# Two kinds of small product regrouped in a two-layer hybrid attention block: the block compression in four groups of eight, the compressed branch's values in one 128-row product a head

## The chip, the cores and the metric

The kernel runs on one core of a Trainium2 chip. The metric is the device time of one execution in microseconds (us), the median of three runs. The core has five engines with queues of their own: TensorE (PE in the profile, its weight loads shown as PEld), VectorE (DVE), ScalarE (ACT), GpSimd (POOL) and SyncE (SP), which issues nearly all of this kernel's DMAs.

## The reference, cut to what matters

Two layers of width 1024 over 512 tokens, each with two attention mixers, a gated sum of them, and an MLP. The mixer that the change touches is the second one: eight query heads of 64 dimensions in two groups of four, each group with its own keys and values, and three branches whose outputs are added under gates. The first branch attends to compressed keys and values: 31 overlapping blocks of 32 tokens, each put through a two-layer network.

```python
def compress_blocks(t, pos_emb, w1, b1, w2, b2):
    blocks = t[:, :, idx, :] + pos_emb            # 31 blocks of 32 tokens
    flat = blocks.reshape(B, G, nc, CMP_BLOCK * dh)   # 2048 numbers a block
    return jax.nn.gelu(flat @ w1 + b1) @ w2 + b2
...
    s = einsum('bgrqd,bgnd->bgrqn', qi, kc) * scale
    p_c = softmax(where(valid_c, s, NEG_BIG)) * valid_c
    o_c = einsum('bgrqn,bgnd->bgrqd', p_c, vc)
...
    o_n = g[..., 0:1] * o_c + g[..., 1:2] * o_s + g[..., 2:3] * o_w
```

It is done for keys (w1[0]) and for values (w1[1]) of both groups. In the other mixer, the log of the forget gates is summed along the tokens (`cumsum`).

## The kernel before, in words

Activations lie transposed, features on the 128 partitions and the 512 tokens along the free axis. Most products keep float32 accuracy by splitting each operand into a high and a low float32r part and adding three products, high by high, high by low, low by high (`gemm`, L212 to L214). Weights come as 128x1024 float32 chunks by DMA (`fetch`, L170), are split by ScalarE (L186, high) and VectorE (L187, low), and are used in a fixed order, a few chunks ahead.

Attention runs in `attend`: three stages of neighbouring heads are interleaved, scores (L392 and L395, with the softmax's maximum on VectorE, L398, and its exponential on ScalarE, L399), transposes of the probabilities (L421, split by L430 on ScalarE and L431 on VectorE) and products with the values (L447). Between their steps a "fill" generator does other work: in the first mixer, the projections of the next heads and the compression; in the second mixer, the compressed branch's probabilities and the gate projections. So the order in which Python yields decides roughly what lies beside what, and the language's scheduler settles the order on each engine's queue when the program is built. It may also move a DMA issue far ahead, up to the point at which its buffer is free.

Compression (`compress`, L498 to L577). VectorE copies the projected keys and values into tiles `ca` (L506 to L511, L508 writes the position rows). Then 32 products (L525) accumulate in one PSUM bank: for each of 8 steps c, two 256-KB chunks of w1 are loaded (L520, into buffers of the tags `oh` and `ol`, of which there are eight each, shared with the query copies `qx` and with the outputs of finished pairs of heads), and for two values of j and two of i (keys, values) a plain float32 product of 128 rows, 64 columns and 256 moving elements is added: keys to partitions 0 to 63, values to 64 to 127. After each j the generator yields, so that another piece of fill, six products of a projection, comes between. The hidden layer, its GELU and the second layer follow (L532 to L577). The values end as `vc2`, 128 rows (the same 32 blocks four times, one for each head of the group) by 2 groups by 128 columns, high parts in columns 0 to 63 and low parts in 64 to 127 (L576 on ScalarE, L577 on VectorE).

The compressed branch's probabilities (`cmp_probs`) of the four heads of a group come out as one 128x512 tile, row 32r+n for head r and block n: scores L586, transposes L593, the softmax on VectorE and ScalarE (L596 to L608), transposes back L612, and the split into `ch` (L615, ScalarE) and `cl` (L616, VectorE).

Each head of the second mixer ends in `after`: two products (L815) take rows 32r to 32r+31 of `vc2`, against the same rows of `ch` and of `cl`, 32 rows by 128 columns by 512 moving elements each, and add to the head's accumulator, which already holds the other two branches. `out_half` (L458 ScalarE, L459 VectorE) then adds the lower 64 partitions to the upper ones.

Three smaller places. `setup` clears the padded key tile `kcz` on GpSimd (L637). `forget` (L661, L662) sums the gates with float32 products whose moving operand is a 128x128 tile of ones. `go` makes that tile (L1083) and uses it for ten warm-up products as well (L1087).

Of the kernel before, what the change touches and what calls it, by code (L numbers as in the profile page):

```python
# [11 lines left out]
F32 = mybir.dt.float32  # L12
F32R = mybir.dt.float32r
AF = mybir.ActivationFunctionType
# [5 lines left out]
T = 512  # L20
# [123 lines left out]
class Body:  # L144
    def __init__(self, ctx, tc, nc, a):
# [5 lines left out]
        self.dp = P("dp", 1, space=bass.MemoryType.DRAM)  # L151

    BUFS = dict(raw=2, wh=2, wl=2, uh=8, ul=8, oh=8, ol=8, va=4, kd=2, q2=3, vn=1, e=2, t2=12, tmp=3,
                hl=1, r=1, crs=1, small=1, cc=1, s4=6, big=1, kcz=1, vc2=1, g4=2)
# [343 lines left out]
    def compress(self, kc, vc, small, l):  # L498
# [14 lines left out]
            A.append(t)  # L513
            yield
        hp = self.p("O")
        for c in range(8):
            w = []
            for i in range(2):
                raw = self.t(("oh", "ol")[i], [128, T], name="w1")
                nc.sync.dma_start(raw, a["w1"][l, i, c].rearrange("p j m -> p (j m)"))  # L520
                w.append(raw)
            for j in range(2):
                jj = 2 * c + j
                for i in range(2):
                    nc.tensor.matmul(hp[64 * i:64 * i + 64, :256], A[i][jj // 8][:, jj % 8],  # L525
                                     w[i][:, j * 256:(j + 1) * 256], start=jj == 0, stop=jj == 15)
                yield
        h = self.t("tmp", [128, 256])
        nc.scalar.copy(h, hp[:, :256])
        pt = self.p("S")  # L530
# [41 lines left out]
        b2v = small[:, OFF["b2v"]:OFF["b2v"] + 64]  # L572
        for hk in range(2):
            nc.vector.scalar_tensor_tensor(v[:, hk], pv[:, hk * 64:hk * 64 + 64], 0.5, b2v, op0=OP.mult, op1=OP.add)
        self.vc2 = self.t("vc2", [128, 2, 128], F32R)
        nc.scalar.copy(self.vc2[:, :, :64], v)  # L576
        nc.vector.tensor_sub(self.vc2[:, :, 64:], v, self.vc2[:, :, :64].bitcast(F32))  # L577

    def cmp_probs(self, hk, q2):

        nc = self.nc
        sc = self.p("S")
        for r in range(4):
            q = q2[2 * hk + r // 2][:, r % 2]
            for f in range(2):
                nc.tensor.matmul(sc, self.kcz[:, hk, f, 96 - 32 * r:224 - 32 * r], q,  # L586
                                 start=r == 0 and f == 0, stop=r == 3 and f == 1)
        s = self.t("tmp", [128, T])
        nc.scalar.copy(s, sc)
        pt = self.p("PT")  # L590
        for b in range(NB):
            sl = slice(b * 128, (b + 1) * 128)
            nc.tensor.transpose(pt[:, sl], s[:, sl], self.ident)  # L593
# [12 lines left out]
        gt = self.gates[:, :, 0, 4 * hk:4 * hk + 4]  # L606
        nc.vector.tensor_mul(z.rearrange("p (b r) -> p b r", b=NB), z.rearrange("p (b r) -> p b r", b=NB), gt)
        nc.vector.tensor_mul(x3, x3, z[:, :, None].to_broadcast([128, 16, 32]))  # L608
        pt = self.p("PT")
        for b in range(NB):  # L610
            sl = slice(b * 128, (b + 1) * 128)
            nc.tensor.transpose(pt[:, sl], x[:, sl], self.ident)  # L612
        h = self.t("t2", [128, T], F32R, name="ch")
        lo = self.t("t2", [128, T], F32R, name="cl")
        nc.scalar.copy(h, pt)  # L615
        nc.vector.tensor_sub(lo, pt, h.bitcast(F32))  # L616
        self.pc[hk] = (h, lo)
        yield

    BUFS.update(s16=2)  # L620
# [18 lines left out]
    def forget(self, z):  # L639

# [65 lines left out]
    def layer(self, l, u):  # L706
# [99 lines left out]
        def nsa_units(h):  # L806
# [2 lines left out]
            O = [None]  # L809

            def after():
                ph, pl = self.pc[hk]
                s = slice(32 * r, 32 * r + 32)
                for f, t in enumerate((ph, pl)):
                    nc.tensor.matmul(O[0], self.vc2[s, hk], t[s], start=False, stop=f == 1)  # L815
# [262 lines left out]
    def go(self):  # L1078
        nc, a = self.nc, self.a
        self.gain = self.cp.tile([128, 40], F32, name="gain")  # L1080
        nc.sync.dma_start(self.gain, a["gain"])
        self.ones = self.cp.tile([128, 128], F32, name="ones")
        nc.vector.memset(self.ones, 1.0)  # L1083
        self.ones2 = self.ones[:, :2]
        ps = self.p("PT")
        for _ in range(self.WARM):
            nc.tensor.matmul(ps[:, :128], self.ones, self.ones, start=True, stop=True)  # L1087
        warm = self.t("s4", [128, 1], name="warm")
        nc.scalar.activation(warm, self.ones[:, :1], AF.Exp)
# [211 lines left out]
```

## Time and profile before

| | us |
|---|---|
| median of three runs | 1553.21 (1552.73 to 1553.71) |
| the profiled execution | 1552.95 |
| span of the program in it | 1551.2 |
| outside the span | 1.75 |

The profile is of one execution. Its first part gives each engine's busy time. The other views used below are the chain of work that ended last, the table of who waited for whom, the timeline of single engines (start, length, engine, line, output and inputs, shape, how many merged), the instructions of one line (shortest, median and longest duration in ns), and busy times by stage. A matrix product's length in the timeline reaches over the start of the next one, since products are pipelined, so its cost on TensorE is read from one start to the next. A plain float32 product appears as two records, a float32r product as one.

### The profile page before, as it was taken

Reading aid. Unit: us, or ns where it says so; the run is one execution under the profiler, and the core shown is the slowest. Engines: PE = TensorE matmul, PEld = TensorE weight load, DVE = VectorE, ACT = ScalarE, POOL = GpSimd, SP = SyncE. Lnnn points to the kernel's source line nnn. Section 1 sums busy time; section 2 is a strip of 40 time slices with the busy share of each in tenths; the row PEclk is TensorE's granted clock in tenths of the full one; section 3 lists DMA queues with packets and bytes.
Section 4 is the critical chain, followed back from the end, with each engine's and each line's share of the span. In section 5 each row is a group of like instructions: output and inputs, shape, how many; then the busy total and the mean of one; then the engine's idle time right before and its main releaser. Section 6 shows DMA issues by size and latency. Waiting matters only on the chain.

```text
span 1551.2 us, 22739 instructions
## 1 busy us (share of the span) xinstructions
PE 1536.4 (99%) x8460; PEld 1306.6 (84%) x8460; DVE 1075.2 (69%) x2204; ACT 776.0 (50%) x1455; POOL 205.2 (13%) x177
## 2 busy tenths in 40 slices
PE   9999999999999999999999999999999999999997
PEld 8877888888888999999887688888888889999997
DVE  5687988766569776664646789887664887766643
ACT  6444655553454555444433456555434635545553
POOL 4000000000201232221400000000002013222222
PEclk9999999999999999999999999999999999999999
DMA  7545422133333322321535543221433333323131
GB/s 240 172 128 154 127 82 82 55 114 117 96 95 123 109 96 95 109 82 64 176 117 165 157 140 100 68 82 55 150 95 95 95 120 99 113 91 99 65 96 55
DMA packets 56638, 169.57 MB, mean 109 GB/s; under 512 B 7344, under 2 KB 8112, under 8 KB 56528
## 3 DMA queue, kind: packets, MB, share of 16 engines
q1 hardware_dynamic: 53072, 161.84, 33.5%
q10 hardware_dynamic: 3456, 6.29, 1.2%
q8 instruction: 66, 1.08, 0.3%
q14 instruction: 44, 0.36, 0.1%
HBM read 140.77 MB, written 4.19 MB: 93 GB/s over the span
## 4 chain that ended last, share of the span: by engine, by line
PE 95%; DVE 3%; ACT 1%; issue 1%; POOL 0%; DMA 0%; DVEq 0%; SPq 0%; POOLq 0%; ACTq 0%
PE ps_mm L212 12%; PE ps_mm L213 12%; PE ps_mm L214 12%; PE ps_S L1196 4%; PE ps_O L1196 4%; PE ps_O L447 4%; PE ps_mm L1196 3%; PE ps_PT L421 3%; PE ps_PT L1196 3%; PE ps_S L212 3%; PE ps_S L213 3%; PE ps_S L214 3%; PE ps_PT L212 3%; PE ps_PT L213 3%; PE ps_PT L214 3%; PE ps_O L212 3%
## 5 line engine op out<-in xcount | busy, mean ns | idle before, releaser
L186 ACT CAST wh<-raw 128x1024 fp32r<-128x1024 f32 (+2 forms) x187 | 192.6, 1030 | 263.7 <-issue 58.5
L187 DVE TENSOR_TENSOR wl<-raw,wh 128x1024 fp32r<-128x1024 f32 (+2 forms) x187 | 226.6, 1212 | 49.8 <-ACT wh L186 48.9
L212 PE MATMUL ps_mm<-uh,wh 128*128 128x512 f32 x512 | 205.1, 401 | 0.0
L214 PE MATMUL ps_mm<-uh,wl 128*128 128x512 f32 x512 | 202.3, 395 | 0.0
L213 PE MATMUL ps_mm<-ul,wh 128*128 128x512 f32 x512 | 202.1, 395 | 0.0
L399 ACT ACTIVATE E<-E,mx 128x128 f32<-128x128 f32 x192 | 108.0, 563 | 82.7 <-DVE mx L398 75.6
L430 ACT CAST pth<-ps_PT 128x512 fp32r<-128x512 f32 x144 | 73.0, 512 | 94.7 <-PE ps_PT L421 94.4
L212 PEld LDWEIGHTS ps_mm<-uh,wh 128*128 128x128 f32 x512 | 96.2, 188 | 26.5 <-issue 10.6
L214 PEld LDWEIGHTS ps_mm<-uh,wl 128*128 128x128 f32 x512 | 96.2, 188 | 20.4 <-issue 0.8
L213 PE MATMUL ps_mm<-ol,wh 128*128 128x512 f32 (+1 forms) x288 | 111.5, 387 | 1.5 <-POOL ol L1263 1.5
L212 PE MATMUL ps_mm<-oh,wh 128*128 128x512 f32 (+1 forms) x288 | 111.8, 388 | 0.0
L214 PE MATMUL ps_mm<-oh,wl 128*128 128x512 f32 (+1 forms) x288 | 111.2, 386 | 0.0
L398 DVE CUSTOM_DVE_ANT_0 E<-ps_S,ct 128x128 f32<-128x128 f32 x192 | 92.2, 483 | 26.5 <-PE ps_S L395 25.0
L213 PEld LDWEIGHTS ps_mm<-ul,wh 128*128 128x128 f32 x512 | 96.4, 188 | 15.1
L431 DVE TENSOR_TENSOR ptl<-ps_PT,pth 128x512 fp32r<-128x512 f32 x144 | 85.0, 595 | 27.6 <-ACT pth L430 27.2
L1187 DVE TENSOR_TENSOR sl<-s,sh 128x512 fp32r<-128x512 f32 x96 | 76.6, 801 | 36.6 <-ACT sh L1186 36.3
L1263 POOL TENSOR_TENSOR ol<-c,oh 128x512 fp32r<-128x512 f32 x48 | 62.7, 1306 | 295.9 <-ACT oh L1262 268.3
L1186 ACT CAST sh<-raw 128x512 fp32r<-128x512 f32 x72 | 44.7, 620 | 106.3 <-PE ps_S L1196 48.1
L1186 ACT CAST sh<-s 128x512 fp32r<-128x512 f32 x96 | 59.3, 620 | 56.4 <-PE ps_PT L1196 19.3
L253 POOL TENSOR_TENSOR acc<-sq 128x512 f32<-128x512 f32 (+1 forms) x6 | 8.4, 1394 | 595.0 <-DVE wl L187 580.1
L421 PE MATMUL ps_PT<-ct,E 128*128 128x128 f32 x480 | 82.9, 273 | 1.4 <-DVE ptl L431 1.4
L421 PEld LDWEIGHTS ps_PT<-ct,E 128*128 128x128 f32 x480 | 60.1, 140 | 14.8 <-DVE ptl L431 4.2
(441 smaller groups left out, 4068.0 us busy)
## 6 DMA issues: line engine op xcount, KB each, us to landing
raw<-wb SPq DMA_DIRECT2D x64, 512.0 KB, 3.2
raw<-wup SPq DMA_DIRECT2D x64, 512.0 KB, 3.7
raw<-wd SPq DMA_DIRECT2D x48, 512.0 KB, 3.5
kd<-hl SPq DMA_DIRECT2D x48, 256.0 KB, 4.6
w<-w SPq DMA_DIRECT2D x32, 256.0 KB, 5.8
q<-hl SPq DMA_DIRECT2D x64, 128.0 KB, 3.2
raw<-wo SPq DMA_DIRECT2D x16, 512.0 KB
raw<-wout SPq DMA_DIRECT2D x16, 512.0 KB, 3.6
```

The costliest lines, as they stand in the source:

```text
L186: nc.scalar.copy(h[:, :n], raw[:, :n])
L187: nc.vector.tensor_tensor(lo[:, :n], raw[:, :n], h[:, :n].bitcast(F32), op=OP.subtract)
L212: mm(ps, h[:, c], xh, start=start and i == 0, stop=False)
L213: mm(ps, h[:, c], xl, start=False, stop=False)
L214: mm(ps, lo[:, c], xh, start=False, stop=stop and i == ks - 1)
L398: nc.vector.tensor_tensor_reduce(e, ps[:, :n], self.mask[:, T - n:], -1.0, BIG, OP.add, OP.min, mx)
L399: nc.scalar.activation(e, e, AF.Exp, bias=mx, scale=-1.0, accum_out=sm[:, i:i + 1])
L421: nc.tensor.transpose(ps[:, j * 128:(j + 1) * 128], E[i][:, b * 128:(b + 1) * 128], self.ident)
L431: nc.vector.tensor_sub(lo[:, o:o + n], ps[:, :n], h[:, o:o + n].bitcast(F32))
L1186: nc.scalar.copy(h, src)
L1187: nc.vector.tensor_tensor(lo, src, h.bitcast(F32), op=OP.subtract)
L1196: self.nc.tensor.matmul(ps, w, x, skip_group_check=True, **kw)
```

## The change

It does four things.

1. In `compress`, the chunks of w1 are loaded two steps ahead, and the products come in four groups of eight (two steps c at a time: four j, two i each) without a yield inside a group. The number of yields is the same as before, 16.
2. The compressed values go into a tile `vz` of 128 rows by 2 groups by 2 by 128 columns that is cleared once on GpSimd. Of its two versions, one holds the value rows of heads 0 and 2 of a group and zeros between, the other those of heads 1 and 3. Four copies on ScalarE and four subtractions on VectorE of 32 partitions each write it, in place of one and one of 128 partitions.
3. The probabilities are split into two tiles of 128 rows in place of `ch` and `cl`: in the first, rows 0 to 63 are the high parts of heads 0 and 1 and rows 64 to 127 their low parts; in the second it is heads 2 and 3, with the halves the other way round. Two copies and two subtractions of 64 partitions write them, in place of one and one of 128. So each head needs one product of 128 rows, where it had two of 32 rows.
4. The 128x128 tile of ones is no longer kept. The warm-up uses a passing one, and `forget` reads one column of ones, repeated 128 times by a zero stride.

```diff
+        loaded = deque()
+
+        def load(c):
+            for i in range(2 if c < 8 else 0):
                 raw = self.t(("oh", "ol")[i], [128, T], name="w1")
                 nc.sync.dma_start(raw, a["w1"][l, i, c].rearrange("p j m -> p (j m)"))
-                w.append(raw)
-            for j in range(2):
+                loaded.append(raw)
+
+        load(0)
+        load(1)
+        for c in range(0, 8, 2):
+            load(c + 2)
+            yield
+            load(c + 3)
+            yield
+            w = [loaded.popleft() for _ in range(4)]
+            for j in range(4):
                 jj = 2 * c + j
                 for i in range(2):
                     nc.tensor.matmul(hp[64 * i:64 * i + 64, :256], A[i][jj // 8][:, jj % 8],
-                                     w[i][:, j * 256:(j + 1) * 256], start=jj == 0, stop=jj == 15)
-                yield
+                                     w[j // 2 * 2 + i][:, j % 2 * 256:(j % 2 + 1) * 256],
+                                     start=jj == 0, stop=jj == 15)
+            yield
+            yield
...
-        self.vc2 = self.t("vc2", [128, 2, 128], F32R)
-        nc.scalar.copy(self.vc2[:, :, :64], v)
-        nc.vector.tensor_sub(self.vc2[:, :, 64:], v, self.vc2[:, :, :64].bitcast(F32))
+        for k in range(4):
+            s = slice(32 * k, 32 * k + 32)
+            z = self.vz[s, :, k % 2]
+            nc.scalar.copy(z[:, :, :64], v[s])
+            nc.vector.tensor_sub(z[:, :, 64:], v[s], z[:, :, :64].bitcast(F32))
...
-        h = self.t("t2", [128, T], F32R, name="ch")
-        lo = self.t("t2", [128, T], F32R, name="cl")
-        nc.scalar.copy(h, pt)
-        nc.vector.tensor_sub(lo, pt, h.bitcast(F32))
-        self.pc[hk] = (h, lo)
+        self.pc[hk] = []
+        for f in range(2):
+            c = self.t("t2", [128, T], F32R, name="cp")
+            s, o = (slice(64 * e, 64 * e + 64) for e in (f, 1 - f))
+            nc.scalar.copy(c[s], pt[s])
+            nc.vector.tensor_sub(c[o], pt[s], c[s].bitcast(F32))
+            self.pc[hk].append(c)
...
+        self.vz = self.cp.tile([128, 2, 2, 128], F32R, name="vz")
+        nc.gpsimd.memset(self.vz.bitcast(F32), 0.0)
...
-                nc.tensor.matmul(ps[:8, s], p[:, k * 8:(k + 1) * 8], self.ones, start=k == 0, stop=False)
+                nc.tensor.matmul(ps[:8, s], p[:, k * 8:(k + 1) * 8], self.ones2[:, :1].to_broadcast([128, 128]), start=k == 0, stop=False)
...
-                ph, pl = self.pc[hk]
-                s = slice(32 * r, 32 * r + 32)
-                for f, t in enumerate((ph, pl)):
-                    nc.tensor.matmul(O[0], self.vc2[s, hk], t[s], start=False, stop=f == 1)
+                nc.tensor.matmul(O[0], self.vz[:, hk, r % 2], self.pc[hk][r // 2], start=False, stop=True)
...
-        self.ones = self.cp.tile([128, 128], F32, name="ones")
-        nc.vector.memset(self.ones, 1.0)
-        self.ones2 = self.ones[:, :2]
+        self.ones2 = self.cp.tile([128, 2], F32, name="ones")
+        nc.vector.memset(self.ones2, 1.0)
+        ones = self.t("tmp", [128, 128], name="ones")
+        nc.vector.memset(ones, 1.0)
...
-            nc.tensor.matmul(ps[:, :128], self.ones, self.ones, start=True, stop=True)
+            nc.tensor.matmul(ps[:, :128], ones, ones, start=True, stop=True)
```

More of the change, by code (lines that the diff above doesn't have):

```diff
@@ L153 @@
     BUFS = dict(raw=2, wh=2, wl=2, uh=8, ul=8, oh=8, ol=8, va=4, kd=2, q2=3, vn=1, e=2, t2=12, tmp=3,
-                hl=1, r=1, crs=1, small=1, cc=1, s4=6, big=1, kcz=1, vc2=1, g4=2)
+                hl=1, r=1, crs=1, small=1, cc=1, s4=6, big=1, kcz=1, g4=2)
     def t(self, tag, shape, dt=F32, name=None):
@@ L515, in compress @@
         hp = self.p("O")
-        for c in range(8):
-            w = []
-            for i in range(2):
+        loaded = deque()
+        def load(c):
+            for i in range(2 if c < 8 else 0):
                 raw = self.t(("oh", "ol")[i], [128, T], name="w1")
                 nc.sync.dma_start(raw, a["w1"][l, i, c].rearrange("p j m -> p (j m)"))
-                w.append(raw)
-            for j in range(2):
+                loaded.append(raw)
[8 more added lines that the diff above has]
+            for j in range(4):
                 jj = 2 * c + j
@@ L1081, in go @@
         nc.sync.dma_start(self.gain, a["gain"])
-        self.ones = self.cp.tile([128, 128], F32, name="ones")
-        nc.vector.memset(self.ones, 1.0)
-        self.ones2 = self.ones[:, :2]
+        self.ones2 = self.cp.tile([128, 2], F32, name="ones")
+        nc.vector.memset(self.ones2, 1.0)
+        ones = self.t("tmp", [128, 128], name="ones")
+        nc.vector.memset(ones, 1.0)
         ps = self.p("PT")
         for _ in range(self.WARM):
-            nc.tensor.matmul(ps[:, :128], self.ones, self.ones, start=True, stop=True)
+            nc.tensor.matmul(ps[:, :128], ones, ones, start=True, stop=True)
         warm = self.t("s4", [128, 1], name="warm")
-        nc.scalar.activation(warm, self.ones[:, :1], AF.Exp)
+        nc.scalar.activation(warm, ones[:, :1], AF.Exp)
         self.xs = [self.dp.tile([128, T], F32, name=f"xs{k}") for k in range(KT)]
```

## The prediction

> **What bounds the kernel now.** I read the page first (busy times, then the chain that ended last), and after it the table of what TensorE waited for.
>
> ```profile
> PE 1536.4 (99%) x8460; PEld 1306.6 (84%) x8460; DVE 1075.2 (69%) x2204; ACT 776.0 (50%) x1455; POOL 205.2 (13%) x177
> ...
> PE 95%; DVE 3%; ACT 1%; issue 1%; POOL 0%; DMA 0%; DVEq 0%; SPq 0%; POOLq 0%; ACTq 0%
> ```
>
> ```profile
> PE ps_mm L213 <- POOL ol L1263: 1.5, 2, 1.1
> PE ps_O L525 <- DVE ca L511: 1.4, 2, 0.7
> PE ps_PT L421 <- DVE ptl L431: 1.4, 2, 0.7
> ```
>
> TensorE makes up 95% of the chain, and the longest waits that end its idle time add up to a few microseconds in the whole span; the rows left out are shorter. So the kernel is a queue of products, and time on TensorE that goes away, goes from the end, as long as nobody else becomes late. The two last rows lie in the compression, once a layer, and come back below. A busy share of 99% hides something, though: what a product costs is the distance from its start to the next start, and around the changed products that distance is longer than elsewhere.
>
> **The values of the compressed branch (L815).** The timeline of TensorE around one head:
>
> ```profile
> 216.38 0.39 PE L213 MATMUL ps_mm<-ul,wh 128*128 128x512 f32 x1
> 216.61 0.39 PE L214 MATMUL ps_mm<-uh,wl 128*128 128x512 f32 x1
> 216.93 0.49 PE L815 MATMUL ps_O<-ch,vc 32*128 32x512 f32 x1
> 217.26 0.39 PE L815 MATMUL ps_O<-cl,vc 32*128 32x512 f32 x1
> 217.58 0.50 PE L212 MATMUL ps_mm<-uh,wh 128*128 128x512 f32 x1
> 217.92 0.40 PE L213 MATMUL ps_mm<-ul,wh 128*128 128x512 f32 x1
> ```
>
> Two 128-row products of 512 columns are 0.23 us apart (216.38 to 216.61). The product ahead of the 32-row pair takes 0.32 to the next start, the pair 0.33 and 0.32, and the product behind it 0.34 (217.58 to 217.92). A head therefore costs 0.09 + 0.65 + 0.11 = 0.85 us. The changed kernel has one 128-row product of the same 512 columns with no change of shape around it: 0.23. It saves 0.62 a head, and with 16 heads in two layers **9.9 us**. As the weights are zero in 64 of the rows, the sum is the same; that zeros cost nothing extra follows from the shape, which is that of the rows beside it.
>
> The Trainium skill speaks against this edit ("TensorEngine Tiling (Array Packing)", Theoretical Speedup): with 32 rows the array splits in four, for a speedup of up to 4. If the two 32-row products ran beside each other they would cost about the 0.23 of one, and the edit would save only the 0.20 around them, 3.2 us. The trace decides otherwise here: both use the same 32 rows, and they start 0.33 us apart.
>
> **The compression products (L525).** One unit of today, both i of one j, in its place:
>
> ```profile
> 94.82 0.39 PE L214 MATMUL ps_mm<-uh,wl 128*128 128x512 f32 x1
> 95.14 0.65 PE L525 MATMUL ps_O<-w,ca 128*64 128x256 f32 x4
> 95.72 0.50 PE L212 MATMUL ps_mm<-uh,wh 128*128 128x512 f32 x1
> 96.05 0.39 PE L213 MATMUL ps_mm<-ul,wh 128*128 128x512 f32 x1
> ...
> 118.00 0.39 PE L213 MATMUL ps_mm<-ul,wh 128*128 128x512 f32 x1
> 118.32 1.08 PE L525 MATMUL ps_O<-w,ca 128*64 128x256 f32 x6
> 119.33 0.50 PE L214 MATMUL ps_mm<-uh,wl 128*128 128x512 f32 x1
> ...
> 120.77 0.65 PE L525 MATMUL ps_O<-w,ca 128*64 128x256 f32 x2
> 121.34 0.50 PE L395 MATMUL ps_S<-kd,qx 128*128 128x512 f32 x1
> 121.68 0.28 PE L447 MATMUL ps_O<-pth,vf 128*128 128x256 f32 x1
> ```
>
> Entry +0.09 (0.32 in place of 0.23), the unit 0.58 (95.14 to 95.72), exit +0.10 (0.33 in place of 0.23): 0.77. What the group looks like is read from two rows. A unit of four records (both i) and one of two records (one i alone, 120.77) take 0.57 to 0.58 alike, so the two i, which write different halves of the columns, run side by side. The row of six records is one unit and one more product: 1.01 to the next start, so one more product behind the first costs 0.43, with entry and exit paid once. If the two i also run side by side further in, a group of four j costs 0.58 + 3 x 0.43 + 0.19 = 2.06, and four groups **8.2 us** a layer.
>
> Today's cost of a layer: 12 undisturbed units at 0.78 (9.4) and one half unit at 117.08 like them (0.8); the stretch 118.00 to 121.68, 3.68 less four 512-column products at 0.23, is 2.8 (one such product and a half unit stand in the rows left out); and the first unit, which stands in a stall:
>
> ```profile
> 86.38 0.40 PE L214 MATMUL ps_mm<-uh,wl 128*128 128x512 f32 x1
> 86.70 0.65 PE L525 MATMUL ps_O<-w,ca 128*64 128x256 f32 x2
> 88.03 0.55 PE L421 MATMUL ps_PT<-ct,E 128*128 128x128 f32 x3 [0.68 <-DVE ptl L431]
> 88.33 0.48 PE L395 MATMUL ps_S<-kd,qx 128*128 128x256 f32 x2
> 89.53 0.65 PE L525 MATMUL ps_O<-w,ca 128*64 128x256 f32 x2 [0.71 <-DVE ca L511]
> 90.11 0.39 PE L447 MATMUL ps_O<-pth,vf 128*128 128x256 f32 x1
> ```
>
> 86.38 to 90.11 is 3.73, of which the other products need 0.8 and L447 behind pays 0.1: 3.0. Together 9.4 + 0.8 + 2.8 + 3.0 = 16.0. In the order of the changed program (read from the built program, no time is in it) all four groups stand unbroken, and the first comes two dozen projection products later, so the wait for `ca` goes. The wait for `ptl` stays and grows: L421 still cannot start before 88.03, and TensorE now arrives at 86.61, so 1.4 us of idle time stand where 0.6 of product stood. Saved: 16.0 - 8.2 - 1.4 = 6.4 a layer, **12.8 us** in two.
>
> **What is added beside it.** The smaller pieces, by form, from the instructions of single lines:
>
> ```profile
> L577 DVE TENSOR_TENSOR vc<-tmp,vc x2: 278/278/278, 148.1 to 913.0; 128x128 fp32r<-128x128 f32 x2
> L616 DVE TENSOR_TENSOR cl<-ps_PT,ch x4: 692/694/694, 187.9 to 1025.7; 128x512 fp32r<-128x512 f32 x4
> L459 DVE TENSOR_TENSOR o<-ps_O,tmp x32: 673/689/695, 94.5 to 1120.9; 64x512 f32<-64x512 f32 x32
> ```
>
> L459 does 64 partitions in the 0.69 us in which L616 does 128, so halving or quartering the partitions shortens nothing. VectorE gets 3 x 0.28 + 2 x 0.69 = 2.2 us a layer more. ScalarE gets as many instructions more, and is busy half the time. All of it is hidden if VectorE has room. By stage:
>
> ```profile
> 138.00:160.00 22.00, 22.00 (x117) 18.41 (x115) 20.26 (x58) 9.26 (x21) 0.00 (x0) 1.00 0.53 149
> 160.00:200.00 40.00, 40.00 (x219) 33.81 (x218) 38.17 (x101) 26.83 (x61) 0.00 (x0) 1.00 0.38 106
> ```
>
> The columns are length, then busy time of PE, PEld, DVE, ACT and POOL. Between 138 and 200 VectorE is busy 58.4 of 62 us, and 0.8 (`vz`) plus 0.7 (the first group of heads) fall just there: 59.9 of 62. That still fits, barely. The built order makes one thing late there: between the transposes L593 and L612, the program now puts 16 projection products where there are 25.
>
> ```profile
> 179.13 0.66 PE L593 MATMUL ps_PT<-ct,tmp 128*128 128x128 f32 x4
> ...
> 186.65 0.60 PE L612 MATMUL ps_PT<-ct,tmp 128*128 128x128 f32 x4
> ```
>
> ```profile
> 185.47 0.68 DVE L608 TENSOR_TENSOR tmp<-tmp,s 128x512 f32<-128x512 f32 x1
> ```
>
> TensorE reaches L612 7.5 us after L593 today; nine products at 0.23 less make that 5.5, while the softmax on VectorE ends at 186.15, 7.0 after L593, and its order there is unchanged. So TensorE waits 1.5 us, in both layers: **+3.0 us**. The bounds are 0 (if L593 itself comes later against VectorE's work) and 6 (if the whole of VectorE's added 1.5 also shows).
>
> The rest at nothing, with bounds. The w1 loads are as many as before:
>
> ```profile
> w<-w SPq DMA_DIRECT2D x32, 256.0 KB, 5.8
> ```
>
> Twelve instead of eight are issued before the projections' weights in each layer, 1 MB more, in a place where SyncE waits for free buffers anyway; a late chunk would show as a wait of TensorE, and I allow 1 us a layer. Clearing `vz` is one more instruction among the clears at the start, on an engine that is busy 13%. The products in `forget` read a repeated column; there are six a layer, of two records each. No row shows a repeated moving operand. I take no change, since the shape is the same. At worst twice as slow, it would be 24 x 0.11 = 2.6 us, with the step of the L421 records above, which also have 128 columns (three take 0.30, 88.03 to 88.33).
>
> **The sum.** -9.9 - 12.8 + 3.0 = -19.7. The profiled execution took 1552.95, 0.26 less than the median of the runs, so I forecast 1552.95 - 19.7 + 0.26, that is **1533.5**.
>
> **The rivals.**
> 1. VectorE becomes the bound of the stretch 138 to 200 in each layer. For it: 59.9 of 62. Against: TensorE waits for nobody there now. If the added 2.2 us a layer show in full on top of the wait at L612, it costs 4.4, and with 1 us a layer for products that meet a busy VectorE after the compression has shrunk, 6.4: 1538 to 1540. Chance 0.25.
> 2. The wait at L612 does not come, since the scheduler's shift of those nine products only moves them ahead of L593: 1530.5, and with the whole `ptl` wait of 2 x 1.4 hidden as well, 1528. Chance 0.18.
> 3. The change doesn't do what it says: inside a group the two i stop running side by side, since nothing in the trace shows a second pair directly behind a first. Each group is then 0.58 + 7 x 0.43 + 0.19 = 3.8, four of them 15.1, and the compression saves -0.5 a layer instead of 6.4: 1547. Against it: in the row of six, the third product starts while the order alternates i. Chance 0.05.
> 4. Slower than before: TensorE, which takes its queue in order, stands at the fourth group for the last four chunks of w1, since SyncE issues these behind the query copies of the third pair of heads. They are first issued about 6 us after that projection ends and land about 6 later, and the group stands some 25 us behind the projection, by the order and 0.23 a product. Each microsecond beyond the 13 of slack costs 2 in all; it outweighs the saving from 10 us beyond it. The chunks would have to take four times today's 5.8. Chance 0.02.
>
> **How the numbers follow.** The forecast (1531 to 1537) has 0.47, rival 1 has 0.25, rival 2 0.18, rival 3 0.05, rival 4 0.02, and 0.03 is left for an order whose stalls eat the gain. The range from 1528 to 1541 takes in the forecast, rivals 1 and 2, and the bounds of the repeated column; what it leaves out is under 0.2. A change of 0.2%, 3.1 us, is about what a measurement of this kernel can tell from none. Faster by more than that: the first four, 0.95. Same 0.02, slower 0.03.
>
> **What would show it.** The value products: 16 of 128 rows, each 0.23 from start to start, no 0.32 ahead. The compression: four rows of 16 records a layer, about 1.87 to the next start; 3.6 would be rival 3. A wait of TensorE (or its weight loads) at L612 of about 1.5, twice; at L421 of 1.4, twice; none for `ca`. VectorE at 96% or more between 138 and 200 with waits of TensorE on L398 or L431 is rival 1. The forecast is wrong if the stretch from 86 to 138 shrinks by less than 5 us.

## The result and the profile after

| | before | after |
|---|---|---|
| median, us | 1553.46 (4 runs, 1552.73 to 1553.89) | 1544.12 (4 runs, 1543.45 to 1546.21) |
| the profiled execution, us | 1552.95 | 1544.18 |
| its span, us | 1551.2 | 1542.1 |

The ratio is 0.9943, with a 95% interval of 0.9925 to 0.996. The kernel is 9.3 us faster. The forecast was 1533.5, within 1528 to 1541: the sign was right, but of the 19.7 us that it expected less than half came, and the time lies outside the range.

The page of the changed kernel has the same two lines as that of before, busy times and chain:

```profile
PE 1520.6 (99%) x8444; PEld 1307.0 (85%) x8444; DVE 1078.6 (70%) x2215; ACT 779.9 (51%) x1465; POOL 207.8 (13%) x178
...
PE 91%; DVE 6%; ACT 2%; issue 1%; DMA 1%; POOL 0%; DVEq 0%; SPq 0%; POOLq 0%; ACTq 0%
```

TensorE's busy time fell by 15.8 us, the span by 9.1. The difference went to waits: TensorE's part of the chain fell from 95% to 91%, and VectorE's rose from 3% to 6%. The table of TensorE's waits in the changed kernel (total, times, longest) says at which lines:

```profile
PE ps_mm L212 <- DVE gate L854: 3.1, 2, 1.5
PE ps_PT L421 <- DVE ptl L431: 2.5, 2, 1.2
PE ps_S L392 <- DVE mx L398: 1.8, 4, 0.6
...
PE ps_S L601 <- DMA q<-hl: 0.4, 1, 0.4
```

The wait for `ca` is gone. The waits for `ptl` grew from 1.4 to 2.5. New are the waits for the gate (3.1), for the maxima L398 (1.8), and some shorter ones, of which the one for a DMA is shown.

The products themselves are what the forecast said. TensorE's timeline of the changed kernel, around the first group of the compression (L535, formerly L525), around one head's value product (L831, formerly L815), at L566, behind the compression's hidden layer (L554 before), and at the transposes L627 (L612 before):

```profile
94.00 0.39 PE L214 MATMUL ps_mm<-uh,wl 128*128 128x512 f32 x1
94.32 1.95 PE L535 MATMUL ps_O<-w,ca 128*64 128x256 f32 x16
96.20 0.50 PE L212 MATMUL ps_mm<-uh,wh 128*128 128x512 f32 x1
96.53 0.40 PE L213 MATMUL ps_mm<-ul,wh 128*128 128x512 f32 x1
...
138.71 0.55 PE L566 MATMUL ps_S<-G,small 128*128 128x64 f32 x3 [0.15 <-DVE G L556]
...
184.17 0.60 PE L627 MATMUL ps_PT<-ct,tmp 128*128 128x128 f32 x4
...
214.32 0.39 PE L214 MATMUL ps_mm<-uh,wl 128*128 128x512 f32 x1
214.55 0.40 PE L831 MATMUL ps_O<-cp,vz 128*128 128x512 f32 x1
214.78 0.39 PE L212 MATMUL ps_mm<-uh,wh 128*128 128x512 f32 x1
```

A group is one row of 16 records and 1.88 to the next start (94.32 to 96.20), with 0.09 ahead and 0.10 behind: 2.07 where 2.06 was forecast. The value product costs 0.23 (214.55 to 214.78). So neither product is the reason.

Where the time comes and goes is read by comparing the starts of the same product in both kernels. In the kernel before, L554 is here:

```profile
143.44 0.66 PE L554 MATMUL ps_S<-G,small 128*128 128x64 f32 x4
```

The compression stage of the first layer has therefore gained 143.44 - 138.71 = 4.7 us, where 6.4 were forecast. At the transposes L612 (186.65 before, 184.17 now) the lead is down to 2.5, at the end of the layer's attention it is 4.4, and in the second layer the same happens once more, to 9.1 at the end of the span. The second mixer, which was to bring 4.95 - 1.5 a layer, brings about nothing.

### The profile page after: what moved, and what is told of

It reads as the page before. It is cut to its first block, busy times and chain, and to the rows that moved or that the text cites. A ratio compares the mean times of both kernels' runs of the same rounds, so it can differ in the third digit from the quotient of the medians.

```text
span 1542.1 us, 22729 instructions
## 1 busy us (share of the span) xinstructions
PE 1520.6 (99%) x8444; PEld 1307.0 (85%) x8444; DVE 1078.6 (70%) x2215; ACT 779.9 (51%) x1465; POOL 207.8 (13%) x178
## 4 chain that ended last, share of the span: by engine, by line
PE 91%; DVE 6%; ACT 2%; issue 1%; DMA 1%; POOL 0%; DVEq 0%; SPq 0%; POOLq 0%; ACTq 0%
PE ps_mm L212 11%; PE ps_mm L213 11%; PE ps_mm L214 11%; PE ps_S L1213 4%; PE ps_O L1213 4%; PE ps_O L447 4%; PE ps_mm L1213 3%; PE ps_PT L1213 3%; PE ps_PT L421 3%; PE ps_S L212 3%; PE ps_S L213 3%; PE ps_S L214 3%; PE ps_PT L212 3%; PE ps_PT L213 3%; PE ps_PT L214 3%; PE ps_O L213 3%
## 5 line engine op out<-in xcount | busy, mean ns | idle before, releaser
L212 PE MATMUL ps_mm<-uh,wh 128*128 128x512 f32 x512 | 203.1, 397 | 0.0
L430 ACT CAST pth<-ps_PT 128x512 fp32r<-128x512 f32 x144 | 73.0, 511 | 91.8 <-PE ps_PT L421 91.4
L212 PE MATMUL ps_mm<-oh,wh 128*128 128x512 f32 (+1 forms) x288 | 111.9, 389 | 3.2 <-DVE gate L854 3.1
L212 PEld LDWEIGHTS ps_mm<-uh,wh 128*128 128x128 f32 x512 | 96.3, 188 | 18.0 <-ACT E L399 1.5
L398 DVE CUSTOM_DVE_ANT_0 E<-ps_S,ct 128x128 f32<-128x128 f32 x192 | 91.4, 481 | 22.5 <-PE ps_S L395 21.6
L431 DVE TENSOR_TENSOR ptl<-ps_PT,pth 128x512 fp32r<-128x512 f32 x144 | 85.0, 593 | 26.4 <-ACT pth L430 25.8
L421 PE MATMUL ps_PT<-ct,E 128*128 128x128 f32 x480 | 85.2, 275 | 2.9 <-DVE ptl L431 2.5
L421 PEld LDWEIGHTS ps_PT<-ct,E 128*128 128x128 f32 x480 | 60.3, 141 | 17.9 <-DVE ptl L431 5.5
```

The costliest lines, as they stand in the source:

```text
L212: mm(ps, h[:, c], xh, start=start and i == 0, stop=False)
L398: nc.vector.tensor_tensor_reduce(e, ps[:, :n], self.mask[:, T - n:], -1.0, BIG, OP.add, OP.min, mx)
L421: nc.tensor.transpose(ps[:, j * 128:(j + 1) * 128], E[i][:, b * 128:(b + 1) * 128], self.ident)
L431: nc.vector.tensor_sub(lo[:, o:o + n], ps[:, :n], h[:, o:o + n].bitcast(F32))
```

## The experiments

**The theories.** A: the loss comes from the pieces that the two splits add (eight instructions of 32 partitions for the values, two and two of 64 for each group's probabilities), although VectorE had room for their time. Its rival B puts the loss elsewhere: into what the regrouped compression brings on behind it, or into the value products themselves. The first three kernels take the change apart. All medians below stand beside runs of the kernel before on the same chip, whose medians were 1553.28 to 1553.66.

### Each part alone

The first kernel is before with the new loop of `compress` only (the diff of that function, nothing else).

> Only the four groups of eight, with the values as in the kernel before. The trace of the changed kernel shows the compression stage 5.0 us a layer shorter, and 5.4 us a layer lost again in the second mixer. Theory A (the added instructions of the split, on VectorE and ScalarE, delay what TensorE waits for): without them the loss in the second mixer is at most the 1.7 us wait behind the compressed softmax, so 10.0 - 3.4 = 6.6 to 10 us faster than before. Theory B (the loss comes with the products' new places: TensorE is early and meets VectorE's chain, and the order of the second mixer is settled anew): the loss is here too, 4 to 5 us a layer, so 0 to 2 us faster.

Measured: 1543.73 (1543.55 to 1545.18), ratio 0.9941 [0.9928, 0.9953], 9.6 faster: as fast as the whole change. In it the lead of 4.7 us at the end of the compression stands unchanged through the second mixer. So the loss behind the compression isn't the compression's doing. Its table of waits already holds two of the three new rows, with the same numbers: 2.5 for `ptl` and 1.8 for the maxima.

The second is the changed kernel with the loop of before in `compress`.

> Only the 128-row value product, its split and the ones; the compression as before. Products save 0.59 us x 16 = 9.4 us. Theory A: the split's instructions cost about 3.7 us a layer, so 2 us faster than before. Theory B: the order of the second mixer stays nearly that of before, so 8 to 9 us faster.

Measured: 1553.26 (1552.76 to 1554.36), ratio 1.0 [0.9991, 1.0009]. The value part, forecast at 9.9 less 3.0, gains nothing at all, less even than the 2 us that theory A left it. It has the third new row:

```profile
PE ps_mm L212 <- DVE gate L842: 3.1, 2, 1.5
```

The third is before, with the splits cut and the products unchanged:

```diff
-        nc.scalar.copy(self.vc2[:, :, :64], v)
-        nc.vector.tensor_sub(self.vc2[:, :, 64:], v, self.vc2[:, :, :64].bitcast(F32))
+        for k in range(4):
+            s = slice(32 * k, 32 * k + 32)
+            nc.scalar.copy(self.vc2[s, :, :64], v[s])
+            nc.vector.tensor_sub(self.vc2[s, :, 64:], v[s], self.vc2[s, :, :64].bitcast(F32))
...
-        nc.scalar.copy(h, pt)
-        nc.vector.tensor_sub(lo, pt, h.bitcast(F32))
+        for f in range(2):
+            s = slice(64 * f, 64 * f + 64)
+            nc.scalar.copy(h[s], pt[s])
+            nc.vector.tensor_sub(lo[s], pt[s], h[s].bitcast(F32))
```

> The kernel before with all its products, but the split of the compressed values written by four plus four instructions of 32 partitions, and that of the probabilities by two plus two of 64, as in the changed kernel: the added instructions alone. Theory A: 4 to 7 us slower than before. Theory B: within 1 us of before.

Measured: 1559.28 (1558.9 to 1559.92), ratio 1.0039 [1.0026, 1.0051], 6.0 slower, with the gate's wait:

```profile
PE ps_mm L212 <- DVE gate L842: 3.1, 2, 1.6
```

The cut alone costs 6.0 us without any of the new products: A stands, and B falls for the regrouping. VectorE got 4.4 us of instructions more; the cut costs more than its own time. ScalarE got as many pieces more, and no kernel here tells its pieces from VectorE's by moving them.

### Which of the two splits, and by what

In the built program the order of TensorE's queue differs between these kernels. Between the transposes L593 and L612 of the first group of heads stand 33 products in the kernel before, and 24 in the changed kernel and in both kernels above that have the gate's wait. So A has two forms. A1: the pieces matter by the order that they lead to. A2: by their time on VectorE. Four kernels: before with only the values' split cut (first half of the diff above), before with only the probabilities' split cut (second half), the changed kernel with whole instructions for `vz`, and the changed kernel with VectorE's four pieces moved to GpSimd (`nc.gpsimd.tensor_sub`).

> The kernel before, with only the split of the compressed values cut in four pieces of 32 partitions (four copies on ScalarE and four subtractions on VectorE in place of one of each); the result and all products are the same. It adds 3 x 0.28 = 0.84 us a layer on VectorE, and in the built order 24 products instead of 33 stand between the transposes of the scores (L593) and those of the probabilities (L612) of the first group of heads, as in the changed kernel; behind the other group it is 29 in both. Theory A1 (the loss hangs on the order that these pieces lead to: TensorE arrives early at L612 and waits there for the gates' row, 1.5 us a layer, and arrives early behind it): 3.5 to 5 us more than before, 1557 to 1558.5, with a wait of TensorE for the gate of 3 us in all. Theory A2 (each added instruction costs its own time on a full VectorE, whatever the order): 1.7 more, 1555. Theory B (the split is not the cause): 1553.

Measured: 1557.27 (1556.74 to 1557.97), ratio 1.0026 [1.0016, 1.0036]: 3.8 slower, as A1 has it and more than twice the 1.7 of VectorE's time. Its table has `PE ps_mm L212 <- DVE gate L840` with 3.1, twice.

> The kernel before, with only the split of the probabilities cut in two halves of 64 partitions (two copies and two subtractions a group in place of one of each); the result and all products are the same. It adds 2 x 0.69 = 1.4 us a layer on VectorE; between L593 and L612 of the first group stand 33 products in the built order, as before. Theory A1 (the order decides): 0 to 2 us more than before, 1553.3 to 1555.5, without a wait for the gate. Theory A2 (each added instruction costs its own time): 2.8 more, 1556. Theory B: 1553.

Measured: 1556.84 (1556.09 to 1557.33), ratio 1.002 [1.0011, 1.0029]: 3.4 slower, which is A2's 2.8 and a little, and A1's forecast missed. The gate's wait is not there. The one row of its table that belongs to the second mixer's new work:

```profile
PE ps_PT L593 <- ACT tmp L589: 0.2, 1, 0.2
```

The waits are too short for the table, but the starts of the same products in both kernels show where the time goes. L612 starts at 186.65 before and at 187.04 here, a transpose L421 behind it at 193.85 before and at 195.03 here: 0.8 us are lost in these 7 us. Behind the second group of heads it is 0.5, and the second layer loses the same again at the same places. That is right behind the pieces, and about as much as one piece of 0.69 on VectorE for each group, as A2 has it. But TensorE's order changes there too (from 188.9 on), and ScalarE has a piece more as well, so which of the three makes the loss is open.

The masked version, with `zm` a 128x2 tile that holds a one where the version has its rows and a zero elsewhere, set once on GpSimd:

```diff
-        for k in range(4):
-            s = slice(32 * k, 32 * k + 32)
-            z = self.vz[s, :, k % 2]
-            nc.scalar.copy(z[:, :, :64], v[s])
-            nc.vector.tensor_sub(z[:, :, 64:], v[s], z[:, :, :64].bitcast(F32))
+        for e in range(2):
+            z, m = self.vz[:, :, e], self.zm[:, e:e + 1]
+            nc.scalar.activation(z[:, :, :64], v, AF.Copy, scale=m)
+            nc.vector.scalar_tensor_tensor(z[:, :, 64:], v, m, z[:, :, :64].bitcast(F32), op0=OP.mult, op1=OP.subtract)
```

> The changed kernel, but the two versions of the compressed values are written whole: each by one copy on ScalarE with a column of ones and zeros as its scale and one scalar-tensor-tensor on VectorE (value times the column, less the high part) over 128 partitions, two and two instructions in place of four and four, and no clearing of the tile. The same products as the changed kernel; 32 of them stand between L593 and L612 of the first group in place of 24. Theory A1: the gate's wait goes and with it about 2.5 us a layer; 1538 to 1541. Theory A2: half of the added pieces goes, 2 x 2 x 0.28 = 1.1 less, 1543. Theory B (the 128-row value products lose their gain themselves, or give it back at the end of each head): 1544, with the gate's wait gone and others in its place.

Measured: 1539.7 (1539.4 to 1540.06), ratio 0.9913 [0.99, 0.9927]: 4.4 less than the changed kernel, as A1 has it; A2's 1.1 alone is out. Its table has no row for the gate and begins with the 2.5 for `ptl` and the 1.8 for the maxima. So 3.1 of the 4.4 us are the gate's wait.

> The changed kernel, with the four subtractions that write the low parts of the compressed values on GpSimd in place of VectorE (all operands lie in SBUF). VectorE loses 4 x 0.28 = 1.1 us a layer; 26 products in place of 24 stand between L593 and L612 of the first group in the built order, so the order stays nearly that of the changed kernel. Theory A1 (order): the gate's wait stays for the most part, 1.0 to 1.5 a layer; 1542 to 1544. Theory A2 (VectorE's time): 2.2 less, 1542, and with VectorE freed of more than the cut added 1541. Theory B: 1544.

Measured: 1545.24 (1543.98 to 1545.52), ratio 0.9946 [0.9933, 0.9958]. VectorE is freed of all four pieces, more than the values' cut added there, and nothing is gained; the median is 1.1 us above the changed kernel's, above all three forecasts. (That it is slower isn't shown: the profiled run has a single wait of 1.5 us of TensorE, at 873 us, for which the profile shows no releaser, and two of the five runs took 1543.98.) 26 products stand between the transposes, and the wait stays, shorter by the two products that came back (2 x 0.23 in each layer):

```profile
PE ps_mm L212 <- DVE gate L854: 2.2, 2, 1.1
```

So for the values' split A1 holds: with 24 or 26 products between the transposes TensorE arrives before the gate, and with 32 or 33 it does not. The pieces' time on VectorE has no part in this wait, since VectorE ends the gate equally late behind the transposes in every kernel. The first transposes, the gate on VectorE, and the product L212 that waits for it or not, in the kernel before (its transposes start at 179.13), in the changed kernel (transposes alone) and in the masked version:

```profile
184.87 0.68 DVE L838 TENSOR_TENSOR gate<-ps_mm,R 128x512 f32<-128x512 f32 x1
```

```profile
176.91 0.64 PE L608 MATMUL ps_PT<-ct,tmp 128*128 128x128 f32 x4
```

```profile
174.82 0.66 PE L607 MATMUL ps_PT<-ct,tmp 128*128 128x128 f32 x4
...
180.56 0.68 DVE L857 TENSOR_TENSOR gate<-ps_mm,R 128x512 f32<-128x512 f32 x1
...
181.62 0.39 PE L212 MATMUL ps_mm<-oh,wh 128*128 128x512 f32 x1
```

VectorE ends the gate 6.42 us behind the start of the first transposes before, 6.42 in the masked version, and 6.40 in the changed kernel (182.63 + 0.68 - 176.91, from the rows further down); in all the other kernels it is 6.4 as well. TensorE's products up to L212 fill 7.06 us before and 6.80 in the masked version, but only 4.76 in the changed kernel (181.44 + 0.23 - 176.91), where it stands until the gate is done.

### The value products without the cut

The changed kernel with whole instructions for both splits, to see what the products alone are worth. It leaves out the second version of `vz` and the pairing of high with low parts, so its products multiply the wrong rows; their number, shape and place are those of the changed kernel:

```diff
-        for k in range(4):
...
+        z = self.vz[:, :, 0]
+        nc.scalar.copy(z[:, :, :64], v)
+        nc.vector.tensor_sub(z[:, :, 64:], v, z[:, :, :64].bitcast(F32))
...
+        nc.scalar.copy(h, pt)
+        nc.vector.tensor_sub(lo, pt, h.bitcast(F32))
+        self.pc[hk] = (h, lo)
```

> The changed kernel with the splits as they were before: one copy and one subtraction of 128 partitions each for the compressed values (into the first version of the cleared tile; the second stays zero) and for the probabilities. The products are the same in number, shape and place, one of 128 rows a head; what they multiply is not the right pair of parts, so the compressed branch's output is left wrong in this kernel and only its time is read. 33 products stand between L593 and L612, as before. Theory A1 (the value products gain their 0.6 a head, and the pieces of the two splits and the order they lead to take it back): grouped compression and values in full, 1543.7 - 9.4 = 1534.3; 1533 to 1536. Theory B (the products lose the gain at the end of each head, where something else waits): 1541 to 1544, with waits of TensorE in the second mixer that are not there before.

Measured: 1536.94 (1536.26 to 1538.36), ratio 0.9895 [0.988, 0.991]. That lies between the forecasts, nearer to A1's. Against the regrouping alone the products bring 1543.73 - 1536.94 = 6.8 of the 9.9; the splits cost 1544.12 - 1536.94 = 7.2. Two of the rows of its table that the regrouping alone does not have:

```profile
PE ps_S L599 <- DMA q<-hl: 0.4, 1, 0.4
...
PE ps_mm L212 <- DVE gate L850: 0.3, 2, 0.2
```

With two more (0.3 without a releaser, 0.2 for L556) these rows account for 1.2 of the missing 3.1. The starts of the same products in the two kernels show the places. Every head gains its 0.6 in both layers, but for the fourth, which gains 0.2: there the gate's wait stands. Behind the second head 0.3 is lost again in both layers. Once each, 0.5 is lost at that DMA, 0.5 at the wait without a releaser (871 us) and 0.2 in the first 20 us. Why the second head loses is open, and the last three lie outside the value products.

### The compression's missing 1.4 us a layer

VectorE's timeline between 87 and 92, first of the kernel before, then of the changed one:

```profile
87.29 0.68 DVE L431 TENSOR_TENSOR ptl<-ps_PT,pth 128x512 fp32r<-128x512 f32 x1
...
87.98 1.50 DVE L511 COPY ca<-tmp 64x248 f32<-64x248 f32 x4
...
89.98 0.28 DVE L398 CUSTOM_DVE_ANT_0 E<-ps_S,ct 128x128 f32<-128x128 f32 x1
```

```profile
86.21 1.22 DVE L187 TENSOR_TENSOR wl<-raw,wh 128x1024 fp32r<-128x1024 f32 x1
87.36 0.68 DVE L431 TENSOR_TENSOR ptl<-ps_PT,pth 128x512 fp32r<-128x512 f32 x1
...
88.04 1.51 DVE L511 COPY ca<-tmp 64x248 f32<-64x248 f32 x4
...
90.04 0.28 DVE L398 CUSTOM_DVE_ANT_0 E<-ps_S,ct 128x128 f32<-128x128 f32 x1
```

The queue is the same to 0.07 us. The copies of the values into `ca` still stand ahead of the maxima. What changed is TensorE, which gets there earlier (timeline of the changed kernel):

```profile
89.43 0.40 PE L214 MATMUL ps_mm<-uh,wl 128*128 128x512 f32 x1
90.38 0.45 PE L392 MATMUL ps_S<-kd,q 128*128 128x384 f32 x1 [0.55 <-DVE mx L398]
```

The next score product, at 92.03, waits for its maxima in the same way. From start to start the two cost 90.38 - 89.43 - 0.23 = 0.72 and 92.03 - 91.30 - 0.23 = 0.50, together 1.2 of the 1.6 us that a layer's compression lacks. If that is the cause, it must go when the copies leave VectorE. Four kernels move them. The edit is always in this place, here with half of the copies on ScalarE:

```diff
-                        nc.vector.tensor_copy(t[half][r * 64:(r + 1) * 64, :, h, :31],
-                                              v[h * 64:(h + 1) * 64, r, :, half:half + 31])
+                        copy = nc.scalar.copy if half else nc.vector.tensor_copy
+                        copy(t[half][r * 64:(r + 1) * 64, :, h, :31],
+                             v[h * 64:(h + 1) * 64, r, :, half:half + 31])
```

The first puts the values' copies on GpSimd, in the changed kernel itself (the line meant is L511):

> The changed kernel with the eight large copies of the values' blocks (L526 and behind) on GpSimd in place of VectorE, where they stand ahead of what TensorE waits for between 86 and 92 us. If VectorE's copies are what keeps TensorE waiting there (1.4 + 0.7 + 0.5 us a layer), 2 to 5 us faster than the changed kernel, 1539 to 1542. If something else ends last there, or GpSimd is too slow for the first group, no faster, 1544 or more.

Measured: 1546.28 (1545.45 to 1547.9), ratio 0.9954 [0.9941, 0.9968], 2 slower than the changed kernel. The waits on L398 are gone, but that for `ptl` grew:

```profile
PE ps_PT L421 <- DVE ptl L431: 6.0, 2, 3.0
```

GpSimd's and VectorE's timelines of this kernel show why:

```profile
84.16 6.60 POOL L512 COPY ca<-tmp 64x248 f32<-64x248 f32 x8 [3.00 <-DVE tmp L336]
```

```profile
85.63 2.47 DVE L512 COPY ca<-tmp 64x248 f32<-64x248 f32 x4
88.13 1.51 DVE L187 TENSOR_TENSOR wl<-raw,wh 128x1024 fp32r<-128x1024 f32 x1
89.57 0.68 DVE L431 TENSOR_TENSOR ptl<-ps_PT,pth 128x512 fp32r<-128x512 f32 x1
```

While GpSimd copies, VectorE's four copies of the keys take 2.47 in place of 1.51 and the weight split 1.51 in place of 1.22, so L431 comes 2.2 us later than in the changed kernel (0.4 of it stood before: L336, ahead of the copies, starts at 83.41, in the changed kernel at 82.97).

The next two stand on the masked version (1539.7): the values' copies on ScalarE, and the half of keys and values.

> The changed kernel with the values written by the column of ones and zeros (two and two instructions), and with the eight copies of the values into the compression's tiles on ScalarE in place of VectorE, where they stood ahead of the maxima (L398) of the next head; ScalarE is idle there for 5 us. Theory A1: the 1.8 us of waits on L398 go, so 2 less than the kernel with the column alone (1539.7), 1537 to 1538.5. Rival: the order that follows, or ScalarE's own queue (exponentials L399 behind the copies), takes it back, 1539.5 to 1541.

> As the kernel before this one in the list, but the second half of the copies of both the keys and the values is on ScalarE (eight in all) and the first half stays on VectorE. Theory A1: VectorE reaches L431 1.5 us earlier, so the wait of L421 for it (2.5 in all) goes as well, for part of the waits on L398: 1536.5 to 1538.5. Rival: ScalarE's queue takes it back, 1539.5 to 1541.

Measured: 1538.07 (1536.83 to 1538.51), ratio 0.99 [0.9885, 0.9915], and 1535.89 (1535.33 to 1536.18), ratio 0.9887 [0.987, 0.9903]. As A1 had it, the second a little below its numbers: 1.6 and 3.8 less than the masked version. With the values' copies on ScalarE, no row for L398 is left in the table, and the 2.5 for `ptl` stays: the 1.6 is what these waits (1.8 in the table) were worth. With the half, no row for `ptl` is left and L398 keeps 1.0. The first group of the compression now starts here:

```profile
92.22 0.39 PE L214 MATMUL ps_mm<-uh,wl 128*128 128x512 f32 x1
92.54 1.95 PE L536 MATMUL ps_O<-w,ca 128*64 128x256 f32 x16
```

That is 1.8 us ahead of the changed kernel's 94.32. This is the fastest version, 8.2 us less than the changed kernel. The last kernel puts all sixteen copies on ScalarE.

> As the kernel with half of the copies on ScalarE (1535.9), but all sixteen copies of keys and values into the compression's tiles are on ScalarE. Theory A1: the last 1.0 us of waits on L398 goes, 1534.5 to 1535.5. Rival: sixteen copies of about 0.4 us in ScalarE's queue hold up the exponentials (L399) and the high parts (L430) behind them, 1536.5 to 1540, with waits of TensorE on ScalarE that are not in the other kernel.

Measured: 1543.77 (1542.96 to 1545.13), ratio 0.9939 [0.9925, 0.9952]: the rival, and worse than its numbers. ScalarE's queue, then VectorE's, then the row of the table:

```profile
85.78 5.01 ACT L512 COPY ca<-tmp 64x248 f32<-64x248 f32 x8
90.82 0.86 ACT L430 CAST pth<-ps_PT 128x384 fp32r<-128x384 f32 x2
```

```profile
91.33 0.56 DVE L431 TENSOR_TENSOR ptl<-ps_PT,pth 128x384 fp32r<-128x384 f32 x1 [3.89 <-ACT pth L430]
91.80 0.28 DVE L398 CUSTOM_DVE_ANT_0 E<-ps_S,ct 128x128 f32<-128x128 f32 x1
```

```profile
PE ps_S L392 <- DVE mx L398: 5.3, 2, 2.7
```

Eight copies in a row hold up the high part L430, VectorE stands for it 3.89 us with L431, and the maxima are queued behind L431. The table names VectorE, though VectorE was idle: the cause stands one step further back.

## Why the prediction was wrong, step by step

- **The prices of the products were right.** 2.07 a group for 2.06, and 0.23 a value product for 0.23. That the two halves run side by side within a group (against rival 3) came out as argued from the rows.
- **"So the wait for `ca` goes"** is the step of the compression that failed. The wait went, but the copies that it stood for did not leave VectorE's queue; the maxima L398 behind them became what TensorE met, a wait that the sum put at nothing. The compression brings 9.6 instead of 12.8 (regrouping alone), and of the 3.2 that are missing 2.4 are these waits (1.2 a layer); the rest is not traced. That they are the cause is shown by the values' copies on ScalarE, which take them away and bring 1.6 of it. Half of all the copies there brings 3.8, more than the maxima cost, since the wait at L421 goes too. That wait was predicted at 1.4 and is: 88.09 less 86.45 less 0.23. The prediction's own sign of being wrong came as well: from 86.38 to 143.44 before it is 57.1 us, from 86.45 to 138.71 now 52.3, a shrinking of 4.8, under 5.

```profile
86.45 0.40 PE L214 MATMUL ps_mm<-uh,wl 128*128 128x512 f32 x1
88.09 0.55 PE L421 MATMUL ps_PT<-ct,E 128*128 128x128 f32 x3 [1.24 <-DVE ptl L431]
```

- **"So TensorE waits 1.5 us, in both layers"** was right in size, and in that the nine missing products bring it. The instruction waited for is not the one forecast but its neighbour. The wait shows three products ahead of the transposes (L612 before, L627 now), at L212, which writes the PSUM bank that VectorE's L854, the gate, has to read first; in VectorE's queue L854 stands just ahead of the softmax's last one, L623 (timelines of TensorE and VectorE in the changed kernel):

```profile
181.44 0.39 PE L214 MATMUL ps_mm<-uh,wl 128*128 128x512 f32 x1
183.37 0.50 PE L212 MATMUL ps_mm<-oh,wh 128*128 128x512 f32 x1 [1.54 <-DVE gate L854]
```

```profile
182.63 0.68 DVE L854 TENSOR_TENSOR gate<-ps_mm,R 128x512 f32<-128x512 f32 x1
183.24 0.68 DVE L623 TENSOR_TENSOR tmp<-tmp,s 128x512 f32<-128x512 f32 x1
```

- **"All of it is hidden if VectorE has room"** is the step that failed in the value part. The splits cost 7.2 us, of which 3.0 were in the sum as that wait. The prediction counted VectorE's time and asked whether it fits. It fits: the windows view of the changed kernel has VectorE busy 57.85 of the 62 us between 133 and 195, less than the 96% that rival 1 named (the waits on L398 and L431 that rival 1 also named came, but in the compression). The pieces cost 4.2 more all the same. Those of the values cost 3.8 alone, of which 3.1 are the gate's wait, by another order of TensorE's queue: that is the 3.0 of the sum. Those of the probabilities cost 3.4 alone, without that wait, and the sum had nothing for them: most of the 4.2 is theirs (both cuts together cost 6.0 in the kernel before, a little less than singly). It is lost right behind them; whether by VectorE's time, ScalarE's or the order is open.

```profile
133.00:195.00 62.00, 60.31 (x320) 49.76 (x318) 57.85 (x157) 35.40 (x83) 0.00 (x0) 1.00 0.43 119
```

- **The 9.9 us of the value products** are 6.8 without the splits. The sum took all 16 savings as lying on the path. The products are as cheap as forecast and 14 heads gain their 0.6, but the fourth of each layer loses 0.4 of it to the gate's wait, and behind the second 0.3 is lost again, for a reason that is open. The rest of the 3.1 lies elsewhere in the span (0.5 at a DMA, 0.5 without a releaser, 0.2 at the start).
- **The rest at nothing** holds as far as it can be seen. The products of `forget` with the repeated column take 272 ns each, as before:

```profile
L680 PE MATMUL ps_S<-ones,f x24: 272/272/275, 52.1 to 814.2; 128*8 128x128 f32 x24
```

The three misses, 3.2 + 4.2 + 3.1, are the 10.6 us between forecast and time, to 0.1. They have to add up to about that, since each is the difference of two neighbours in the row before, regrouping alone, no splits, changed kernel. The range was too narrow because its worst case added up only VectorE's own time (4.4, and 1 a layer); none of its cases let the compression, the splits and the value products each lose a part of their gain.

## What to carry to other kernels

Where TensorE is 99% busy, a saved product is worth its price only up to the next thing that another engine has to finish; walk the queue of that engine and ask when it ends if TensorE comes earlier. Small extra instructions are judged not only by whether they fit, but also by the order that the scheduler makes of them: compare the built orders with and without them. Here two whole-width instructions an engine, with a column of ones and zeros as scale, in place of four on slices of the partitions, gained 4.4 us. When copies are moved off a full engine, move as many as the other's idle stretch holds and no more: half gained 3.8 us here, all of them lost 4.1 (both against the masked version).

## What the runs showed of the hardware

- GpSimd's copies and VectorE's instructions that work from SBUF alone shut each other out. Single records of VectorE and GpSimd in the kernel with the values' copies on GpSimd, beside the weight split (88.13, 1.51) shown above:

```profile
86.01 0.70 DVE L512 COPY ca<-tmp 64x248 f32<-64x248 f32 x1
```

```profile
86.52 0.67 POOL L512 COPY ca<-tmp 64x248 f32<-64x248 f32 x1
...
88.61 1.51 POOL L512 COPY ca<-tmp 64x248 f32<-64x248 f32 x1
```

  The GpSimd copy of 86.52 ends 0.48 us behind the VectorE copy that it meets (87.19 and 86.71), the one of 88.61 ends 0.48 behind the split (90.12 and 89.64), so the same copy takes 0.67 beside a short instruction and 1.51 beside a long one. The VectorE copy takes 0.70, where one that is not held up takes 0.36. L431, which reads PSUM as well, took 0.68 in both kernels. The Trainium skill ("SBUF — State Buffer", SBUF: two separate sides) says that the two engines share a pair of SBUF ports, and that whoever holds it shuts the other out for a whole instruction. The trace agrees: the GpSimd copy's length follows that of the instruction it meets.
- The same copy of 64x248 takes 0.38 on VectorE (four in 1.51) and 0.63 on ScalarE (eight in 5.01). On GpSimd the sixteen records go from 0.60 to 1.51, all of them beside work of VectorE, so its time alone is not shown.
